# Differential attention in an fp32 diffusion backbone: the output product spread in groups between the pieces of the projections, with weight tiles of its own, and key copies issued by ScalarE

## Chip, cores, metric

One core of a Trainium2 chip. The metric is the device time of one execution in microseconds (us), lower is better.

## What is computed

The reference runs four layers over 512 latent tokens and 256 context tokens of width 1024: a Fourier mixer, differential attention, latent attention, a Fourier mixer again, each followed by an MLP. Everything is fp32. The change lies in layer 1, differential attention with 8 heads of 2 x 64 query and key channels and 128 value channels:

```python
def diff_attend(q1, q2, k1, k2, v, lam):
    scale = DIFF_HEAD_DIM ** -0.5
    s1 = jnp.einsum("bqhd,bkhd->bhqk", q1, k1).astype(jnp.float32) * scale
    s2 = jnp.einsum("bqhd,bkhd->bhqk", q2, k2).astype(jnp.float32) * scale
    p = jax.nn.softmax(s1, axis=-1) - lam * jax.nn.softmax(s2, axis=-1)
    return jnp.einsum("bhqk,bkhe->bqhe", p.astype(v.dtype), v)
...
    def finish(o):
        b, s = o.shape[:2]
        return (rms_norm(o, subln_g) * (1 - lam_init)).reshape(b, s, D_MODEL) @ w_o
```

Latent queries see all 768 keys, context queries the 256 context keys. `finish` normalises each head's output and multiplies by the output matrix `w_o`; the product, gated, is added to the stream x.

## The kernel before

Activations are kept transposed (channels on partitions, tokens on the free axis), 8 tiles of 128 channels. An fp32 product is made of three fp32r products: each operand is split into a high part (a cast on ScalarE, line 96) and a low part (a subtraction on VectorE, line 97), and hi x hi, hi x lo and lo x hi are summed in PSUM (lines 147 to 154). A weight tile therefore costs a load issued by SyncE (`wload`, line 99), a cast and a subtraction before TensorE can use it. In this stage there are two raw buffers of 512 columns for all loads, and a pool `dw` of eight weight tiles (four weights, high and low).

`diff` walks over the heads. Per head (work on TensorE in the order of the code):

- `S`: scores of one block of 128 queries against all keys, 8 products (12 with a context block), followed by the softmax on VectorE and ScalarE: maximum, exponential with its sum, reciprocals, and the difference of the two maps.
- `Tr`, `T2`: transposes of that difference (six blocks of 128), each split in high and low (`pth`, `ptl`).
- `PVa`: 18 products with the values of 256 queries; `PVb`: a product with ones for the sum of squares, then a chain over ScalarE and VectorE (`nt`, `nr`, `nu`) that ends in the normalised head output, `oh` (high, ScalarE) and `ol` (low, VectorE).

`last(hd - 1, ...)` finishes the second 256 queries of the former head after the first scores of the next one.

Between these stands filling work, which hides the softmax: the projections of values (`v`, for a pair of heads), queries (`q`) and keys (`k`) of later heads, and the output product of a finished pair (`wo`). It waits in a queue, `Fill`. `F(ns)` emits products from its front until that many nominal ns are filled; `need(name)` emits until all pieces of that name are out. Query and key projections come in two pieces (512 latent, 256 context columns, 24 products each); the values of a pair are one generator of 144 products; an output product of a pair is one generator of 96 products: for each of four weights two latent groups of 6 products (512 columns) and one context group of 12 (256 columns). In the queue it comes after the pair's values and the queries and keys of the next head. Each group ends in `accum` (line 368), a VectorE operation that adds it to x. All of this filling work goes through the PSUM tag `w` (`pw` in the profile) with two banks.

A latent key piece goes through the rotary embedding and then `put_k`: casts to `kh` on ScalarE (line 890), a copy of each half to the other 64 partitions by a DMA that GpSimd issues (line 891), and `kl` on VectorE (line 892).

TensorE's order is that of the code; the other engines' orders are made by a scheduler from the same program. TensorE, ScalarE, VectorE and the DMA queues each work in order.

In the rows, `pw<-hhi,g` is a query, `pw<-hhi,whi` a key, `pw<-whi,hhi` a value and `pw<-oh,whi` an output product; `ps` scores, `pu` transposes, value and ones products. Heads are counted from 0, pairs from 1 (heads 0 and 1) to 4.

Of the kernel before, what the change touches and what calls it, by code (L numbers as in the profile page):

```python
# [11 lines left out]
F32 = mybir.dt.float32  # L12
F32R = mybir.dt.float32r
# [31 lines left out]
def body(ctx: ExitStack, tc, a, out):  # L45
# [5 lines left out]
    def pool(es, name, bufs=1, **kw):  # L51
        return es.enter_context(tc.tile_pool(name=name, bufs=bufs, reuse_waits="tile", **kw))
# [39 lines left out]
    def rd(t):  # L92
        return t.bitcast(F32)

    def split(hi, lo, src):
        nc.scalar.copy(hi, src)  # L96
        nc.vector.tensor_sub(lo, src, rd(hi))  # L97
# [65 lines left out]
    class Fill:  # L163

        def __init__(self):
            self.q = []
            self.debt = 0.0
            self.open = False  # L170
            self.held = None

        def add(self, name, gens):
            self.q.extend([name, g, False] for g in gens)
# [14 lines left out]
        def step(self):  # L189
            if not self.open:  # L190
                self.prime(0)
                self.prime(1)
                self.open = True
            c = next(self.q[0][1], None)
            if c is None:
                self.q.pop(0)
                self.open = False
                return 0.0
            return c

        def run(self, ns):
            self.debt += ns
            while self.debt > 0 and self.q and self.q[0][0] != self.held:
                self.debt -= self.step()
            self.debt = min(self.debt, 0.0)

        def need(self, name):
# [3 lines left out]
        def drain(self):  # L211
            while self.q:
                self.step()

    def kview(w, k):
# [587 lines left out]
    def diff(l, h, nm):  # L803
        T = TT
        with ExitStack() as es:
            phase(es, "d", 2, {"s": (1024, 2), "u": (512, 2), "w": (512, 2)}, {"v": 1, "t": 1, "r": 1, "u": 1}, rw=512)
            cp = pool(es, "dc")
            wp = pool(es, "dw", 8)
            sp = pool(es, "ds")
            state["big"] = lambda: sp.tile([128, T], F32, name="big", tag="e0", bufs=2)  # L810
            cos = cp.tile([128, 512], F32, name="dcos")
# [26 lines left out]
                for m, (_, o) in enumerate(halves):  # L838
                    nc.gpsimd.tensor_copy(klz[i][m][o], zt[o])

            def gen_v(pr):
                wv = [wload(wp, a["dwv"][pr, i]) for i in range(4)]
                yield 0.0
                V[pr] = vh, vl = [sp.tile([128, 6, 256], F32R, name=n, tag="v", bufs=2) for n in ("vh", "vl")]
                for t0 in (0, 2, 4):
                    p = pt_("w")
                    for t in range(2):
                        i = 0
                        for k in range(KT):
                            hh, hl = tview(h[k], t0 + t)  # L850
                            wh, wl = tview(wv[k // 2], k % 2, 256)
# [31 lines left out]
            def put_k(hd):  # L883
                kh[hd] = [sp.tile([128, T], F32R, name=f"kh{m}", tag="kh", bufs=4) for m in range(2)]
                kl[hd] = klz[hd % 2]

                def put(t, c0, w_):
                    for m, (r, o) in enumerate(halves):
                        q = kh[hd][m][:, c0:c0 + w_]
                        nc.scalar.copy(q[r], t[r])  # L890
                        nc.gpsimd.dma_start(q[o], q[r])
                        nc.vector.tensor_sub(kl[hd][m][r, c0:c0 + w_], t[r], rd(q[r]))
                return put

# [16 lines left out]
            def gen_wo(pr, norm=None):  # L911
                ws = [wload(wp, a["dwo"][pr, b]) for b in range(2)]
                yield 0.0
                for b in range(4):
# [8 lines left out]
                    for j in range(2):  # L923
                        yield from mm3g(p[:, j * 256:], 2, lambda k: kview(w, k * 2 + j), lambda k: O[2 * pr + k], [(512, 256)], off=512)
                        accum(2 * b + j, 512, 256, p[:, j * 256:(j + 1) * 256], l, G_A)
                        if norm:
                            norm.feed(2 * b + j)

            def S(hd, c0, qi, cqi=None):

                s = [pt_("s"), pt_("s")]
                rows = [(c0 + qi * 128, [(0, 512, 0), (512, 256, 512)], 0, T,
                         [sp.tile([128, T], F32, name=f"e{m}", tag=f"e{m}", bufs=2 - m) for m in range(2)])]
                if cqi is not None:
                    rows.append((SL + cqi * 128, [(SL, SC, 768)], T, SC, [nacc[:, 0:256], nacc[:, 256:512]]))
                for q0, bl, _, _, _ in rows:
                    for m in range(2):
                        for k0, kw, o0 in bl:
                            o = s[m][:, o0:o0 + kw]
                            mm(o, qs[hd][m][:, q0:q0 + 128], kh[hd][m][:, k0:k0 + kw], True, False)  # L940
                            mm(o, qs[hd][m][:, q0:q0 + 128], kl[hd][m][:, k0:k0 + kw], False, True)
                for _, _, o0, w_, e in rows:
                    ri = []
                    for m in range(2):
                        mx = sp.tile([128, 1], F32, name="mx", tag="mx", bufs=4)
                        li = sp.tile([128, 1], F32, name="li", tag="li", bufs=4)
                        sv = s[m][:, o0:o0 + w_]
                        nc.vector.reduce_max(mx, sv, axis=AX.X, negate=True)  # L948
                        nc.scalar.activation(e[m], sv, AF.Exp, bias=mx, accum_out=li)
                        nc.vector.reciprocal(li, li)  # L950
                        ri.append(li)
                    nc.vector.tensor_mul(ri[1], ri[1], lam)
                    nc.scalar.activation(e[1], e[1], AF.Copy, scale=ri[1])
                    nc.vector.scalar_tensor_tensor(e[0], e[0], ri[0], e[1], op0=ALU.mult, op1=ALU.subtract)
                return s, [r[4][0] for r in rows]

            def Tr(e, c0, qi, b):
# [64 lines left out]
                F(1800)  # L1022
                PVb(hd, 256, st)

            fill.add("v0", [gen_v(0)])
            fill.add("q1", gens(1, 1))
            _, (e0, ec) = S(0, 0, 0, 0)
            for hd in range(8):
                p = hd // 2
                w = (5900, 3900, 7000, 7000, 7000, 7000, 7000, 5000)[hd]  # L1030
                F(500)
                if hd:
                    last(hd - 1, e3)
                    if hd % 2 == 0:
                        fill.front(f"v{p}", [gen_v(p)])
                        fill.add(f"wo{p - 1}", [gen_wo(p - 1)])
                F(w - 3500)
                _, (e1,) = S(hd, 0, 1)
                F(0.4 * w)
# [436 lines left out]
```

## Time and profile before

| | us |
|---|---|
| median of 3 runs | 2903.64 (2901.41 to 2911.14) |
| profiled execution | 2903.82 |
| its span, first to last instruction | 2902.0 |
| differential attention's heads, first scores to the last pair's output product | 757 to 1174 |
| TensorE busy in 720 to 1200 (480.0) | 418.38 |
| VectorE busy in the same | 378.94 |
| ScalarE busy in the same | 287.69 |

A window's row gives the busy time and the number of instructions of each engine in a stretch, then the clock granted to TensorE (1.00 is full). A timeline row gives start, duration, engine, line, operation, tiles and, in brackets, how long the engine had been idle and what ended that. A matmul's printed duration overlaps with the next one's; their spacing is the difference of their starts.

### The profile page before, as it was taken

The page shows a single profiled execution, that of the slowest core. Times are in us where ns is not written, and L with a number is a line of the kernel's source. Part 1 is how long each engine was busy: PE and PEld are TensorE (multiplying, and loading weights), DVE is VectorE, ACT ScalarE, POOL GpSimd, SP SyncE. Part 2 cuts the span into 40 slices and gives each one's busy share as a digit, 9 for nine tenths or more (in the row PEclk, how much of TensorE's full clock was granted, in tenths as well). Part 3 has the DMA queues.
Part 4 walks back from the last instruction along what each step waited for, and adds up shares of the span by engine and source line. Part 5 has one row for each costly group of instructions (what it writes and reads, how often), then busy time and mean ns, then how long its engine had stood idle before and what let it go on. Part 6 is the DMA issues. An engine that isn't in the chain of part 4 may idle for free.

```text
span 2902.0 us, 39734 instructions
## 1 busy us (share of the span) xinstructions
PE 2756.0 (95%) x15579; PEld 2377.6 (82%) x15579; DVE 1930.2 (67%) x3390; ACT 1290.8 (44%) x2325; POOL 159.9 (6%) x172
## 2 busy tenths in 40 slices
PE   8999999999799989799999998899899999999998
PEld 5788888888788878688888896788788888788887
DVE  7986666558697788875555448888785555664344
ACT  4542222234475656432332236777553334553342
POOL 0110000002110010100000011000100001100001
PEclk9999999999899999999999998999999999999999
DMA  9454333332111111253333210001265551232231
GB/s 319 148 181 131 110 116 104 107 95 82 48 48 45 40 47 39 96 161 114 120 113 116 88 37 32 22 23 37 71 224 175 163 173 55 81 116 95 80 110 51
DMA packets 93531, 291.12 MB, mean 100 GB/s; under 512 B 10624, under 2 KB 14880, under 8 KB 92832
## 3 DMA queue, kind: packets, MB, share of 16 engines
q1 hardware_dynamic: 90784, 285.44, 30.6%
q0 software_dynamic: 2560, 3.15, 0.5%
q8 instruction: 122, 2.00, 0.3%
q14 instruction: 65, 0.53, 0.1%
HBM read 283.29 MB, written 2.11 MB: 98 GB/s over the span
## 4 chain that ended last, share of the span: by engine, by line
PE 79%; DVE 13%; ACT 4%; issue 1%; DMA 1%; POOL 0%; POOLq 0%; SPq 0%; ACTq 0%; DVEq 0%
PE pw L140 70%; PE pu L140 5%; PE ps L140 3%; DVE x L371 2%; PE pu L797 1%; DVE ptl L97 1%; DVE mx L948 1%; DVE wlo L97 1%; DVE hlo L330 1%; DVE nu L328 1%; DVE mx L1280 1%; ACT e L1283 1%; DVE hlo L348 0%; PE pn L140 0%; ACT pth L96 0%
## 5 line engine op out<-in xcount | busy, mean ns | idle before, releaser
L96 ACT CAST whi<-raw 128x1024 fp32r<-128x1024 f32 (+1 forms) x322 | 308.2, 984 | 1064.7 <-PE pw L140 1012.0
L140 PE MATMUL pw<-hhi,wlo 128*128 128x512 f32 (+2 forms) x1680 | 588.0, 350 | 13.0 <-DVE wlo L97 13.0
L140 PE MATMUL pw<-hhi,whi 128*128 128x512 f32 (+2 forms) x1680 | 591.2, 352 | 3.2 <-ACT whi L96 1.5
L140 PE MATMUL pw<-hlo,whi 128*128 128x512 f32 (+2 forms) x1680 | 589.8, 351 | 0.0
L140 PE MATMUL pw<-ahi,whi 128*128 128x512 f32 (+1 forms) x1664 | 569.1, 342 | 0.0
L140 PE MATMUL pw<-alo,whi 128*128 128x512 f32 (+1 forms) x1664 | 567.6, 341 | 0.5 <-DVE alo L97 0.5
L140 PE MATMUL pw<-ahi,wlo 128*128 128x512 f32 (+1 forms) x1664 | 566.6, 340 | 0.0
L371 DVE SCALAR_TENSOR_TENSOR x<-pw,mod,x 128x512 f32<-128x512 f32 (+1 forms) x504 | 302.1, 623 | 283.0 <-PE pw L140 281.8
L97 DVE TENSOR_TENSOR wlo<-raw,whi 128x1024 fp32r<-128x1024 f32 (+1 forms) x322 | 362.2, 1140 | 164.1 <-ACT whi L96 163.5
L140 PEld LDWEIGHTS pw<-hhi,wlo 128*128 128x128 f32 x1680 | 319.4, 190 | 56.7 <-DVE wlo L97 13.6
L140 PEld LDWEIGHTS pw<-hhi,whi 128*128 128x128 f32 x1680 | 318.8, 190 | 47.7 <-ACT whi L96 1.9
L140 PEld LDWEIGHTS pw<-hlo,whi 128*128 128x128 f32 x1680 | 318.7, 190 | 42.4
L140 PEld LDWEIGHTS pw<-ahi,whi 128*128 128x128 f32 x1664 | 315.5, 190 | 37.0 <-issue 0.2
L140 PEld LDWEIGHTS pw<-alo,whi 128*128 128x128 f32 x1664 | 315.5, 190 | 36.2 <-DVE alo L97 0.7
L140 PEld LDWEIGHTS pw<-ahi,wlo 128*128 128x128 f32 x1664 | 315.1, 189 | 36.1
L264 DVE SCALAR_TENSOR_TENSOR raw<-raw,cb 128x1024 f32<-128x1024 f32 x176 | 216.0, 1228 | 117.2 <-DMA raw<-in_modw 115.5
L264 DVE SCALAR_TENSOR_TENSOR junk<-raw,cb 128x1024 bf16<-128x1024 f32 x96 | 117.2, 1220 | 70.6 <-DMA raw<-in_modw 68.4
L97 DVE TENSOR_TENSOR alo<-r,ahi 128x768 fp32r<-128x768 f32 (+2 forms) x134 | 105.8, 792 | 75.1 <-ACT ahi L96 74.8
L307 POOL TENSOR_TENSOR nacc<-nacc,nsq 128x256 f32<-128x256 f32 x70 | 52.9, 755 | 1751.5 <-ACT nsq L306 1751.2
L97 DVE TENSOR_TENSOR ptl<-pu,pth 128x384 fp32r<-128x384 f32 (+1 forms) x208 | 106.2, 539 | 37.5 <-ACT pth L96 36.0
L797 PE MATMUL pu<-ident,e 128*128 128x128 f32 x576 | 89.1, 280 | 21.1 <-ACT e L1283 11.8
L140 PE MATMUL pw<-hhi,g 128*128 128x512 f32 (+2 forms) x384 | 97.8, 337 | 3.9 <-DVE x L371 2.9
(327 smaller groups left out, 4259.4 us busy)
## 6 DMA issues: line engine op xcount, KB each, us to landing
raw<-in_w SPq DMA_DIRECT2D x252, 512.0 KB, 4.1
raw<-in_modw SPq DMA_DIRECT2D x176, 512.0 KB, 3.7
wm<-in_msh SPq DMA_DIRECT2D x32, 256.0 KB, 6.0
raw<-in_fw SPq DMA_DIRECT2D x10, 512.0 KB, 4.3
cb<-scr SPq DMA_DIRECT2D x4, 1024.0 KB, 5.3
raw<-in_dwk SPq DMA_DIRECT2D x16, 256.0 KB, 2.6
raw<-in_dwq SPq DMA_DIRECT2D x16, 256.0 KB, 2.7
raw<-in_dwv SPq DMA_DIRECT2D x16, 256.0 KB, 2.8
```

Of the source, the lines that this page charges most:

```text
L96: nc.scalar.copy(hi, src)
L97: nc.vector.tensor_sub(lo, src, rd(hi))
L140: r = nc.tensor.matmul(o, lhsT, rhs, start=start, stop=stop)
L264: nc.vector.scalar_tensor_tensor(o, m, 1.0, cb[:, v * 1024:(v + 1) * 1024], op0=ALU.mult, op1=ALU.mult, accum_out=mcol(mod[l, ch], v, k))
L307: nc.gpsimd.tensor_tensor(nacc[:, c0:c0 + w], nacc[:, c0:c0 + w], s, op=ALU.add)
L328: nc.vector.scalar_tensor_tensor(u, xs, am, r, op0=ALU.mult, op1=ALU.mult)
L330: nc.vector.scalar_tensor_tensor(lo, u, sh, rd(hi), op0=ALU.add, op1=ALU.subtract)
L371: nc.vector.scalar_tensor_tensor(xs, src, mcol(mod[l, ch], 0 if c0 < SL else 1, n), xs, op0=ALU.mult, op1=ALU.add)
L797: nc.tensor.transpose(t[:, i * 128:(i + 1) * 128], p[:, (k0 + i) * 128:(k0 + i + 1) * 128], ident)
L948: nc.vector.reduce_max(mx, sv, axis=AX.X, negate=True)
L1280: nc.vector.reduce_max(mx, s[:, :T], axis=AX.X)
L1283: nc.scalar.activation(et, s[:, :T], AF.Exp, bias=mx, scale=MLA_SCALE)
```

## The change

Five edits, all in layer 1:

1. The output product of pairs 1 to 3 leaves the queue and becomes a side generator (`side_wo`) of 12 groups. Whenever a piece of the queue has ended, two whole groups (for the third pair one) are emitted; if the queue is held or empty, `F` emits groups too; before head 3's and head 5's values product, and at the end, what is left is emitted at once (`end_side`). It starts right after `last` of the odd head. The fourth pair's product, after the last head, is as before.
2. The values of a pair become three pieces of 48 products, so that there are more ends of pieces.
3. The side's weights have a pool of their own, `dx`, of two tiles (one weight, high and low), loaded when the first group of the weight is emitted.
4. The key copies are issued by ScalarE instead of GpSimd; the DMA scratch of GpSimd is halved.
5. The two row sums of a softmax share a tile, with one reciprocal for both.

The numbers `w` that `F` is given are changed for head 7 (5000 to 3000).

```diff
@@ class Fill
+            self.side = iter(())
+            self.rate = 2
...
             if c is None:
                 self.q.pop(0)
                 self.open = False
-                return 0.0
+                return sum(next(self.side, 0.0) for _ in range(self.rate))
             return c

         def run(self, ns):
             self.debt += ns
-            while self.debt > 0 and self.q and self.q[0][0] != self.held:
-                self.debt -= self.step()
+            while self.debt > 0:
+                if self.q and self.q[0][0] != self.held:
+                    self.debt -= self.step()
+                else:
+                    c = next(self.side, None)
+                    if c is None:
+                        break
+                    self.debt -= c
             self.debt = min(self.debt, 0.0)
...
+        def end_side(self):
+            for _ in self.side:
+                pass
@@ diff
+            wx = pool(es, "dx", 2)
...
-            def gen_v(pr):
-                wv = [wload(wp, a["dwv"][pr, i]) for i in range(4)]
-                yield 0.0
...
+            def gens_v(pr):
...
+                return [piece(t0) for t0 in (0, 2, 4)]
...
-                        nc.gpsimd.dma_start(q[o], q[r])
+                        nc.scalar.dma_start(rd(q)[o], rd(q)[r])
...
+            def side_wo(pr):
+                for b in range(4):
+                    w = wload(wx, a["dwo"][pr, b])
+                    for j in range(2):
+                        yield wo_lat(pr, w, b, j)
+                    yield wo_cx(pr, w, b)
+
+            def wo_lat(pr, w, b, j):
+                p = pt_("w")
+                mm3(p, 2, lambda k: kview(w, k * 2 + j), lambda k: O[2 * pr + k], [(0, 512)])
+                accum(2 * b + j, 0, 512, p, l, G_A)
+                return 1360.0
+
+            def wo_cx(pr, w, b):
+                p = pt_("w")
+                for j in range(2):
+                    mm3(p[:, j * 256:], 2, lambda k: kview(w, k * 2 + j), lambda k: O[2 * pr + k], [(512, 256)], off=512)
+                    accum(2 * b + j, 512, 256, p[:, j * 256:(j + 1) * 256], l, G_A)
+                return 1440.0
...
-                    ri = []
+                    li = sp.tile([128, 2], F32, name="li", tag="li", bufs=4)
...
-                        nc.vector.reciprocal(li, li)
-                        ri.append(li)
-                    nc.vector.tensor_mul(ri[1], ri[1], lam)
...
+                    nc.vector.reciprocal(li, li)
+                    nc.vector.tensor_mul(li[:, 1:2], li[:, 1:2], lam)
...
-                w = (5900, 3900, 7000, 7000, 7000, 7000, 7000, 5000)[hd]
+                w = (5900, 3900, 7000, 7000, 7000, 7000, 7000, 3000)[hd]
...
-                        fill.front(f"v{p}", [gen_v(p)])
-                        fill.add(f"wo{p - 1}", [gen_wo(p - 1)])
+                        fill.front(f"v{p}", gens_v(p))
+                        fill.side = side_wo(p - 1)
+                        fill.rate = 2 if p < 3 else 1
...
                 if hd in (3, 5):
-                    fill.need(f"wo{p - 1}")
+                    fill.end_side()
```

How this stands on the engines, at three places. First TensorE in head 2, where the latent key piece (`pw` from `hlo`, `hhi`) ends behind the ones product of head 1's second half. Before:

```order
L140 MATMUL pw_7692<-hhi_1751,whi_7652 128x512
L140 MATMUL pu_7798<-nt_7817,ones_79 128x256 [waits Activation_49]
L140 MATMUL pw_7692<-hlo_1752,whi_7652 128x512
L140 MATMUL pw_7692<-hhi_1751,wlo_7653 128x512
L140 MATMUL pw_7881<-hhi_1737,whi_7646 128x256
L140 MATMUL pw_7881<-hlo_1738,whi_7646 128x256
```

After (`oh_7083` is head 0's output, `oh_7538` and `ol_7539` are head 1's):

```order
L140 MATMUL pw_7671<-hhi_1751,whi_7631 128x512
L140 MATMUL pu_7773<-nt_7792,ones_79 128x256 [waits Activation_49]
L140 MATMUL pw_7671<-hlo_1752,whi_7631 128x512
L140 MATMUL pw_7671<-hhi_1751,wlo_7632 128x512
L140 MATMUL pw_7838<-oh_7083,whi_7834 128x512
L140 MATMUL pw_7838<-ol_7084,whi_7834 128x512
L140 MATMUL pw_7838<-oh_7083,wlo_7835 128x512
L140 MATMUL pw_7838<-oh_7538,whi_7834 128x512 [waits Activation_49]
L140 MATMUL pw_7838<-ol_7539,whi_7834 128x512 [waits DVE_49]
L140 MATMUL pw_7838<-oh_7538,wlo_7835 128x512
```

Where the context key piece followed, the first two output groups now stand in between (12 products), and their fourth and fifth products wait for head 1's output.

Second ScalarE in head 4, from the end of the same chain for head 3 (`oh_8722`, `oh_8806`: its output). Before:

```order
L890 CAST kh0_8895<-pw_9083 64x256 [waits DMASW6_49,DMASW4_49,PE_49]
L890 CAST kh0_8895<-qt_9071 64x512 [waits DVE_49]
L890 CAST kh1_8896<-qt_9071 64x512 [waits DMASW7_49,DMASW5_49]
L96 CAST whi_9130<-raw_9128 128x512 [waits DMAHW7_49]
L96 CAST oh_8722<-nu_9068 128x256 [waits DVE_49]
L96 CAST g_9153<-raw_9151 128x512 [waits DMAHW0_49]
L890 CAST kh1_8896<-pw_9083 64x256 [waits DVE_49]
```

After (`whi_9081` is a value weight, `whi_9106` the first output weight of the pair):

```order
L911 CAST kh0_8879<-pw_9034 64x256 [waits PE_49]
L912 DMA kh0_8879<-kh0_8879 64x256 [waits Activation_49]
L911 CAST kh0_8879<-qt_9022 64x512 [waits DVE_49]
L911 CAST kh1_8880<-qt_9022 64x512
L912 DMA kh0_8879<-kh0_8879 64x512 [waits DMAHW6_49,Activation_49]
L912 DMA kh1_8880<-kh1_8880 64x512 [waits DMAHW7_49,Activation_49]
L96 CAST oh_8806<-nu_9019 128x256 [waits DVE_49]
L96 CAST whi_9081<-raw_9079 128x512 [waits DMAHW3_49]
L911 CAST kh1_8880<-pw_9034 64x256 [waits DVE_49]
L96 CAST whi_9106<-raw_9104 128x512 [waits DMAHW5_49]
```

The key copies have entered the row, the value weight's cast has moved behind the head's output, and the output weight's cast is the last of all.

Third TensorE where a context group ends and the next weight's first group follows. Before (second weight of a pair, in head 3):

```order
L140 MATMUL pw_8447<-oh_7557,whi_8286 128x256
L140 MATMUL pw_8447<-ol_7558,whi_8286 128x256
L140 MATMUL pw_8447<-oh_7557,wlo_8287 128x256
L140 MATMUL pw_8497<-oh_7090,whi_8292 128x512
L140 MATMUL pw_8497<-ol_7091,whi_8292 128x512
```

After (the same weight, now in head 2):

```order
L140 MATMUL pw_7934<-ol_7539,whi_7834 128x256
L140 MATMUL pw_7934<-oh_7538,wlo_7835 128x256
L140 MATMUL pw_7955<-oh_7083,whi_7951 128x512 [waits DVE_49,Activation_49]
L140 MATMUL pw_7955<-ol_7084,whi_7951 128x512
L140 MATMUL pw_7955<-oh_7083,wlo_7952 128x512 [waits DVE_49]
```

The next weight's first product waits for its cast and its bank, the third for its subtraction; before, neither waits.

More of the change, by code (lines that the diff above doesn't have):

```diff
@@ L213, in drain @@
                 self.step()
+            self.end_side()
+        def end_side(self):
+            for _ in self.side:
+                pass
     def kview(w, k):
@@ L839, in diff, with piece @@
                     nc.gpsimd.tensor_copy(klz[i][m][o], zt[o])
-            def gen_v(pr):
-                wv = [wload(wp, a["dwv"][pr, i]) for i in range(4)]
-                yield 0.0
-                V[pr] = vh, vl = [sp.tile([128, 6, 256], F32R, name=n, tag="v", bufs=2) for n in ("vh", "vl")]
-                for t0 in (0, 2, 4):
+            def gens_v(pr):
+                st = []
+                def piece(t0):
+                    if not st:
+                        st.extend(wload(wp, a["dwv"][pr, i]) for i in range(4))
+                        V[pr] = [sp.tile([128, 6, 256], F32R, name=n, tag="v", bufs=2) for n in ("vh", "vl")]
+                    yield 0.0
+                    vh, vl = V[pr]
                     p = pt_("w")
@@ L850, in gen_v @@
                             hh, hl = tview(h[k], t0 + t)
-                            wh, wl = tview(wv[k // 2], k % 2, 256)
+                            wh, wl = tview(st[k // 2], k % 2, 256)
                             for u_, v_ in ((hh, wh), (hh, wl), (hl, wh)):
@@ L942, in S @@
                 for _, _, o0, w_, e in rows:
-                    ri = []
+                    li = sp.tile([128, 2], F32, name="li", tag="li", bufs=4)
                     for m in range(2):
                         mx = sp.tile([128, 1], F32, name="mx", tag="mx", bufs=4)
-                        li = sp.tile([128, 1], F32, name="li", tag="li", bufs=4)
                         sv = s[m][:, o0:o0 + w_]
                         nc.vector.reduce_max(mx, sv, axis=AX.X, negate=True)
-                        nc.scalar.activation(e[m], sv, AF.Exp, bias=mx, accum_out=li)
-                        nc.vector.reciprocal(li, li)
-                        ri.append(li)
-                    nc.vector.tensor_mul(ri[1], ri[1], lam)
-                    nc.scalar.activation(e[1], e[1], AF.Copy, scale=ri[1])
-                    nc.vector.scalar_tensor_tensor(e[0], e[0], ri[0], e[1], op0=ALU.mult, op1=ALU.subtract)
+                        nc.scalar.activation(e[m], sv, AF.Exp, bias=mx, accum_out=li[:, m:m + 1])
+                    nc.vector.reciprocal(li, li)
+                    nc.vector.tensor_mul(li[:, 1:2], li[:, 1:2], lam)
+                    nc.scalar.activation(e[1], e[1], AF.Copy, scale=li[:, 1:2])
+                    nc.vector.scalar_tensor_tensor(e[0], e[0], li[:, 0:1], e[1], op0=ALU.mult, op1=ALU.subtract)
                 return s, [r[4][0] for r in rows]
@@ L1023, in last @@
                 PVb(hd, 256, st)
-            fill.add("v0", [gen_v(0)])
+            fill.add("v0", gens_v(0))
             fill.add("q1", gens(1, 1))
@@ L1464 @@
     arrays = _layout({k: np.asarray(v) for k, v in inputs.items()})
-    nc = bacc.Bacc("TRN2", target_bir_lowering=False, num_devices=1, dynamic_dma_scratch_size=8192)
+    nc = bacc.Bacc("TRN2", target_bir_lowering=False, num_devices=1, dynamic_dma_scratch_size=4096)
     feed, aps = {}, {}
```

## The prediction

> **What bounds the kernel now.** I read the page's busy shares and chain first, then the differential-attention stage by head (windows cut at the first score product of each head), then TensorE's waits there, and last the timelines at the places that the change moves.
>
> ```profile
> PE 2756.0 (95%) x15579; PEld 2377.6 (82%) x15579; DVE 1930.2 (67%) x3390; ACT 1290.8 (44%) x2325; POOL 159.9 (6%) x172
> PE 79%; DVE 13%; ACT 4%; issue 1%; DMA 1%; POOL 0%; POOLq 0%; SPq 0%; ACTq 0%; DVEq 0%
> ```
>
> TensorE carries the chain, so the change can only act through TensorE's idle time in this one stage. Columns below: stretch, its length, busy time of PE, PEld, DVE, ACT, POOL, granted clock, DMA. The rows are heads 1 to 6, then head 7 up to its last scores.
>
> ```profile
> 804.20:843.05 38.85, 36.53 (x216) 31.00 (x216) 36.28 (x81) 29.32 (x68) 4.74 (x6) 0.96 0.18 45
> 843.05:897.39 54.34, 51.66 (x360) 47.29 (x360) 43.27 (x92) 35.99 (x81) 4.69 (x6) 1.00 0.18 47
> 897.39:956.91 59.52, 53.02 (x316) 45.59 (x315) 47.13 (x100) 32.59 (x72) 4.67 (x6) 1.00 0.15 42
> 956.91:1010.87 53.96, 49.97 (x350) 45.43 (x349) 43.10 (x90) 35.18 (x80) 5.29 (x6) 1.00 0.17 48
> 1010.87:1069.92 59.05, 52.97 (x316) 45.53 (x315) 46.63 (x100) 32.58 (x72) 4.66 (x6) 1.00 0.15 43
> 1069.92:1124.18 54.26, 50.05 (x351) 45.58 (x350) 43.82 (x92) 36.51 (x83) 5.29 (x6) 1.00 0.19 52
> 1124.18:1158.46 34.28, 29.65 (x179) 26.00 (x178) 28.47 (x65) 19.34 (x45) 0.00 (x0) 0.95 0.08 24
> ```
>
> In heads 2 to 6 TensorE is the fullest engine. In head 1, which has the least product work, VectorE is as full (36.28 of 38.85, 93%). Where TensorE waits:
>
> ```profile
> PE pw L140 <- DVE x L371: 16.7, 16, 2.2
> ```
>
> From 880 to 1160 us the output products wait 16.7 us in 16 waits (1.04 each) for the accumulation into x that frees their bank.
>
> **The parts that take time away.** Three pairs' output products (96 per pair) are respread; pair 3, after the last head, is left alone. Prices:
>
> ```profile
> 940.25:948.82 8.57, 8.57 (x50) 1.00 0.42 107
> L371 DVE SCALAR_TENSOR_TENSOR x<-pw,mod,x 128x512 f32<-128x512 f32 (+1 forms) x60 | 36.3, 612 | 9.7 <-PE pw L140 9.1
> ```
>
> The first is a whole query projection, 24 products of 512 columns and 24 of 256, with two cut ones at its edges: 8.4 us for 48, that is 0.233 and 0.117 each. A pair's output is twice that, 16.8 us.
>
> Heads 3 and 5: by the order, 9 products of 512 columns of a pair (2.1 us) stand in the even head now and the other 14.7 us in the odd one; the changed order has none in heads 3 and 5. So 59.52 falls to 44.8 by the work alone. Head 1 tells what a head without output takes: 38.85, with 12 key products of 512 columns fewer (2.8 us more in heads 3 and 5), and with 3.3 us at half clock (rows below) that cost 1.5. That gives 40.2. VectorE agrees: 47.13 less some 14 accumulations of 0.612 and two weight subtractions is about 37, at head 1's 93% 39.8. Gain beyond the work: 44.8 - 40.2 = 4.6, and 59.05 - 14.7 - 40.2 = 4.2. Sum -8.8 (bounds 0, if 44.8 stays, and -12).
>
> Head 7: it keeps 48 output products (8.4 us) of the 14.5 it has. VectorE loses about 7 accumulations of 0.612, 4.2 of its 28.47; at the present 83% the 34.28 become 29.3, at head 1's 93% 26.1. I take the nearer row, its own: -5.0 (bounds 0 and -8.2). The tail behind it stays, since nothing is left to fill it in either order.
>
> Even heads: three of the 16 waits lie at their ends, 3 x 1.04 = 3.1. And the value pieces of heads 4 and 6 now start before their weights are split (rows of pair 2, below): from the last key product at 967.63 to the scores at 973.00 there are 5.25 us for 21 value products (2.5), 2.8 lost in each. In the new order those weights are ready before the piece starts. Sum -8.7.
>
> Together -22.5.
>
> **The parts that add time.** The first output group of a pair now follows the key piece at once, right behind the ones product of the odd head's second half. In pair 1 it has only the head's normalised output to wait for (4th product on):
>
> ```profile
> 852.52 0.59 PE L140 MATMUL pu<-nt,ones 128*128 128x256 f32 x2
> ...
> 856.72 1.26 ACT L890 CAST kh<-qt 64x512 fp32r<-64x512 f32 x2 [1.18 <-DVE qt L870]
> 858.53 0.40 ACT L96 CAST oh<-nu 128x256 fp32r<-128x256 f32 x1
> ...
> 857.55 0.47 DVE L993 SCALAR_TENSOR_TENSOR nu<-nu,gs,nr 128x256 f32<-128x256 f32 x1
> 859.37 0.42 DVE L97 TENSOR_TENSOR ol<-nu,oh 128x256 fp32r<-128x256 f32 x1
> ```
>
> Two key products of 0.233 and the ones product's own place follow; the group would start at 853.4 and reach its fourth product at 854.1. The cast of the output (oh) ends at 858.93 now, behind one weight cast that the new order has later; without that, and with nu 0.6 earlier, it ends at about 858.4. Wait 4.3, and 0.5 more for ol: 4.8.
>
> In pairs 2 and 3 the group's weight cast stands behind oh, a value-weight cast and a key cast on ScalarE (the order shows it), so the first product already waits:
>
> ```profile
> 966.01 0.59 PE L140 MATMUL pu<-nt,ones 128*128 128x256 f32 x2
> 967.63 0.28 PE L140 MATMUL pw<-hhi,wlo 128*128 128x256 f32 x1
> 973.00 0.39 PE L140 MATMUL ps<-kh,qs 128*128 128x512 f32 x1
> ...
> 971.92 0.68 DVE L97 TENSOR_TENSOR wlo<-raw,whi 128x512 fp32r<-128x512 f32 x1
> 972.52 0.48 DVE L993 SCALAR_TENSOR_TENSOR nu<-nu,gs,nr 128x256 f32<-128x256 f32 x1
> ...
> 973.04 0.41 ACT L96 CAST oh<-nu 128x256 fp32r<-128x256 f32 x1 [1.80 <-DVE nu L993]
> 973.99 0.37 ACT L890 CAST kh<-pw 64x256 fp32r<-64x256 f32 x1
> ```
>
> ```profile
> L96 ACT CAST whi<-raw 128x512 fp32r<-128x512 f32 x47 | 29.0, 623 | 19.6 <-PE pw L140 12.3 <-DMA raw<-in_dwk 3.8 <-DMA raw<-in_dwo 2.1
> L97 DVE TENSOR_TENSOR wlo<-raw,whi 128x512 fp32r<-128x512 f32 x48 | 32.6, 685 | 8.7 <-ACT whi L96 8.3
> ```
>
> The wlo at 971.92 moves behind oh, so nu ends at 972.4 and oh at 972.9; then 0.62, 0.37 and 0.62 on ScalarE: the first product starts at about 974.5 where TensorE was free at 967.75. The low half follows at about 975.4, 0.4 more. 7.1 in each of two pairs, with 4.8: +19.0. The key copies' issues stand ahead of oh on ScalarE too; the 1.80 of idle time there covers two or three of them. Both bounds: with idle queues the same chain is
>
> ```profile
> 1173.74 0.70 PE L140 MATMUL pu<-nt,ones 128*128 128x256 f32 x2 [0.74 <-ACT nu L985]
> ...
> 1177.78 0.50 PE L140 MATMUL pw<-oh,whi 128*128 128x512 f32 x1 [2.65 <-ACT oh L96]
> ```
>
> 4.04 from ones to product: 2.5 in pair 1 and, with 1.61 of casts, 3.9 in the others, 10.3 in all. With today's times unshifted: 21.9. I keep 19.0, since the queues there are today's.
>
> Half clock behind waits (the last column but two is the clock; the first row is from the stage's start, the second from head 1):
>
> ```profile
> 739.89:745.70 5.81, 5.81 (x14) 4.55 (x15) 0.55 (x1) 0.00 (x0) 0.00 (x0) 0.50 0.27 90
> 803.80:807.10 3.30, 2.90 (x9) 2.52 (x10) 3.17 (x7) 1.65 (x4) 0.00 (x0) 0.50 0.01 4
> 1131.50:1134.80 3.30, 3.30 (x17) 3.30 (x16) 1.12 (x3) 1.64 (x6) 0.00 (x0) 0.50 0.00 0
> ...
> 1130.19 0.39 PE L140 MATMUL pw<-oh,whi 128*128 128x256 f32 x1 [2.15 <-DVE x L371]
> ```
>
> A wait of 2.15 us was followed by 3.3 us at half clock (1.7 lost); the longest stretch, with TensorE busy in all of it, was 5.81 (2.9 lost). All three first groups wait longer than 2.15: 1.7 + 2.3 + 2.3, the two long ones between the rows: +6.3 (bounds 5.1 and, with a fourth, 11.6). [...]
>
> Weight tiles of their own: one weight in flight (two tiles). Where a context group ends and the next weight's group follows at once, the cast waits for the former: 0.62 + 0.69 + about 0.2 of hand-over, less two products of 0.233, 1.05 each. That is so three times (heads 2, 4, 4), a half time in head 7 (0.4), and 2.5 at the first in head 2, where the load itself waits until the value weights ahead have left the two raw buffers: +6.0 (bounds 4.2 and 11).
>
> A second group behind a piece needs the bank the piece has just filled: a cast and a subtraction, about 1.5, against 1.4 of the first group, 0.1 to 0.9 in six places; and the group's lump uses up the fill, so that eight transposes in head 2 and a few ones products stand without cover, under 1 each: +4.0 (bounds 0 and 7).
>
> Softmax and key copies:
>
> ```profile
> L950 DVE RECIPROCAL li<-li 128x1 f32<-128x1 f32 x96 | 14.6, 156 | 8.0 <-ACT e L949 5.8 <-ACT nacc L949 1.7
> L891 POOL DMA_DIRECT2D kh<-kh x32 | 16.9, 530 | 39.7 <-ACT kh L890 37.2 <-PE ps L140 1.8
> ```
>
> 48 reciprocals fewer are 7.5 us of VectorE, under 1 a head, and the last one stays in its chain: 0. The copies put 32 x at most 0.53 = 17 us on ScalarE, 2.1 a head, where even head 1 leaves 9.5 idle; heads use their keys a head later, so landing is covered: 0 (bounds -2 and +4; without that idle time the exponentials would be late). Behind a waiting issue stand casts of oh, hence the term above.
>
> **Sum.** -22.5 + 19.0 + 6.3 + 6.0 + 4.0 = +12.8. The profiled execution took 2903.8 (span 2902.0, 1.8 around it), 0.2 above the median of the runs: 2916.6, given as 2916.
>
> **Rivals.**
> A, faster: ScalarE and VectorE empty their queues while TensorE stands, as head 1's 93% suggests they can. Then the first groups cost 10.3, the clock 3.4 (two waits), the tiles 4.2, nothing else, and head 7 gives 8.2 (3.2 more): 2903.8 - 25.7 + 17.9 = 2896. It is under the old time as soon as the new waits stay under 25.7. For it: the waits on x are VectorE's lateness, not TensorE's. Against: in-order queues with the weight cast behind the head's chain. 0.17.
> B, no change: VectorE is drained only at the first groups (10.3 + 5.1), the tiles cost 6.0 and the rest 2: 23.4 against 22.5, 2905. 0.18.
> C, dearer: odd heads and head 7 do not shrink beyond their work, because VectorE or the chain from scores to transposes sets them and ScalarE now has the copies too: 2916.6 + 13.8 = 2930. For it: head 7's tail, slow without fill. 0.15.
> That the groups would not move at all is excluded by the order.
>
> **Numbers.** The forecast keeps 0.50, with 2907 to 2924 as its own range. 0.3% (8.7 us) is about what a measurement of this kernel can tell from no change. Faster than 2895: somewhat less than half of A and tails, 0.11. Within: the rest of A, all of B mostly, and the quarter of the forecast below 2912: 0.34. Slower: 0.55. The range reaches to A and C: 2896 to 2932.
>
> **What would show it.** Right: in the profile after, waits of output products on x shrink from 16.7 to some 4 between the same heads; waits of pw on ACT oh or whi of about 5, 7 and 7 us appear with granted clock 0.5 behind them; heads 3 and 5 take 39 to 41 us, the even ones 70 to 78. Wrong: first-group waits of 3 to 4 us, heads 3 and 5 at 45 or at 36, or ScalarE's issue of a copy far over 0.5 us, which would put exponentials late and TensorE's transposes with them.

## Result and profile after

The changed kernel takes 2940.36 us (median of 4 runs, 2938.98 to 2942.91), the kernel before 2904.82 in the same session (4 runs, 2901.41 to 2911.14). The ratio is 1.0121, 95% interval 1.0105 to 1.0136: slower, as forecast (2916), but by nearly three times as much and above the range (2932). The profiled execution took 2942.9, its span 2940.7, which is 38.7 more than before.

The page's busy shares and the start of its chain, after:

```profile
PE 2773.1 (94%) x15579; PEld 2384.4 (81%) x15579; DVE 1927.5 (66%) x3342; ACT 1289.7 (44%) x2325; POOL 142.5 (5%) x140
PE 78%; DVE 13%; ACT 5%; issue 2%; DMA 2%; POOL 0%; ACTq 0%; POOLq 0%; SPq 0%; DVEq 0%
```

TensorE executes as many products as before (15579). Its busy time is 17 us more, much of it products at half clock (below), which count as longer (with 512 columns their starts lie 0.43 us apart at 853.9 to 855.6, against 0.23 at 847.4 to 847.8); the other 22 us are idle.

The same windows by head, after (columns as in the prediction: length, PE, PEld, DVE, ACT, POOL, clock, DMA). The rows are heads 1 to 6, then head 7 up to its last scores:

```profile
797.87:836.92 39.05, 36.83 (x216) 31.30 (x216) 35.49 (x75) 29.70 (x69) 2.66 (x2) 0.96 0.16 45
836.92:922.18 85.26, 71.16 (x446) 61.09 (x447) 53.64 (x104) 36.70 (x81) 2.56 (x2) 0.98 0.13 36
922.18:964.95 42.77, 38.18 (x231) 32.50 (x230) 35.96 (x76) 30.94 (x71) 2.60 (x2) 1.00 0.16 46
964.95:1054.04 89.09, 72.10 (x437) 62.88 (x436) 58.33 (x109) 39.74 (x87) 3.18 (x2) 0.90 0.14 41
1054.04:1096.55 42.51, 38.06 (x231) 32.14 (x230) 34.50 (x70) 27.39 (x65) 2.67 (x2) 1.00 0.13 34
1096.55:1164.75 68.20, 58.27 (x390) 52.93 (x388) 45.46 (x90) 34.56 (x79) 3.19 (x2) 0.95 0.11 30
1164.75:1192.82 28.07, 23.52 (x143) 20.40 (x141) 25.29 (x54) 20.73 (x48) 0.00 (x0) 0.94 0.18 57
```

Against before, heads 2 to 7 change by +30.9, -16.8, +35.1, -16.5, +13.9 and -6.2. All that stands before head 2 gains 6.1 and what follows the last scores loses 4.3. The products only change heads: priced at 0.233 and 0.117 each, a pair moves 14.7 us from its odd to its even head, and the third pair 6.1 from head 7 to head 6. Length less products (transposes are priced at 0.117 too, which drops out of the differences), the time lost in each head, is then:

| head | lost before | lost after | difference |
|---|---|---|---|
| 2, 4, 6 | 4.4, 6.3, 6.4 | 20.6, 26.8, 14.3 | +44.6 |
| 3, 5 | 8.7, 8.2 | 6.6, 6.3 | -4.0 |
| 7 | 7.5 | 7.4 | -0.1 |

So the loss lies in the even heads, which have the groups, and the odd heads give little back. What TensorE waits for from head 2 to the last scores (us in total, times, longest):

```profile
PE pw L140 <- ACT whi L96: 16.9, 6, 6.9
PE pw L140 <- DVE x L385: 11.5, 13, 1.1
...
PE pw L140 <- DVE wlo L97: 4.8, 3, 2.6
PE pw L140 <- ACT oh L96: 4.2, 1, 4.2
```

(L385 is the accumulation, L371 before.) The waits on x fall from 16.7 only to 11.5, and the waits on casts of weights and output are new. The first groups of the three pairs, from TensorE's timeline:

```profile
852.39 0.50 PE L140 MATMUL pw<-oh,whi 128*128 128x512 f32 x1 [4.16 <-ACT oh L96]
853.30 0.79 PE L140 MATMUL pw<-ol,whi 128*128 128x512 f32 x1 [0.41 <-DVE ol L97]
...
982.61 0.79 PE L140 MATMUL pw<-oh,whi 128*128 128x512 f32 x1 [6.85 <-ACT whi L96]
...
1114.01 0.80 PE L140 MATMUL pw<-oh,whi 128*128 128x512 f32 x1 [6.54 <-ACT whi L96]
```

That is 18.0 us of waits. Why the second takes 6.85 is seen on ScalarE and VectorE (rows of both; TensorE was free at 975.8):

```profile
978.34 1.40 DVE L913 TENSOR_TENSOR kl<-qt,kh 64x512 fp32r<-64x512 f32 x2
979.77 0.48 DVE L1032 SCALAR_TENSOR_TENSOR nu<-nu,gs,nr 128x256 f32<-128x256 f32 x1
...
980.29 0.41 ACT L96 CAST oh<-nu 128x256 fp32r<-128x256 f32 x1 [1.85 <-DVE nu L1032]
980.60 0.61 ACT L96 CAST whi<-raw 128x512 fp32r<-128x512 f32 x1
981.24 0.37 ACT L911 CAST kh<-pw 64x256 fp32r<-64x256 f32 x1
981.94 0.62 ACT L96 CAST whi<-raw 128x512 fp32r<-128x512 f32 x1 [0.33 <-DMA raw<-in_dwo]
```

Two key subtractions hold the head's last normalisation (nu) back, ScalarE's cast of the output stands waiting for nu, and the group's own weight cast is three places behind that cast. This is the queue that the prediction described.

Half clock (the last column but two) goes with each long wait, and with one turn of the weight tiles (the hand-over of the tiles from one weight to the next) in head 4 and one in head 7:

```profile
853.16:856.57 3.41, 3.27 (x8) 2.59 (x9) 0.84 (x2) 0.00 (x0) 0.00 (x0) 0.50 0.21 46
979.45:986.28 6.83, 3.67 (x9) 2.86 (x10) 4.04 (x8) 1.91 (x4) 0.00 (x0) 0.50 0.53 151
1037.48:1047.72 10.24, 8.86 (x33) 7.79 (x34) 3.06 (x6) 3.07 (x8) 0.00 (x0) 0.50 0.08 27
1112.57:1119.40 6.83, 5.39 (x17) 4.53 (x18) 4.24 (x7) 2.58 (x5) 0.00 (x0) 0.50 0.44 119
1180.84:1184.25 3.41, 3.41 (x13) 2.93 (x12) 2.43 (x5) 1.64 (x3) 0.00 (x0) 0.50 0.50 154
```

In the first four stretches TensorE is busy for 21.2 us, half of which, an estimated 10.6, is lost. The fifth, in head 7, costs the 1.7 that head 7 lost to one such stretch before (1131.50 in the prediction's rows), so it adds nothing. The longest follows this turn in head 4, the last weight of the pair (rows of TensorE, ScalarE and VectorE):

```profile
1035.00 0.50 PE L140 MATMUL pw<-oh,whi 128*128 128x512 f32 x1 [1.58 <-ACT whi L96]
...
1038.34 0.79 PE L140 MATMUL pw<-oh,wlo 128*128 128x512 f32 x1 [2.61 <-DVE wlo L97]
...
1033.51 0.94 ACT L992 ACTIVATE e<-e,li 128x768 f32<-128x768 f32 x1 [1.78 <-DVE li L991]
1034.35 0.60 ACT L96 CAST whi<-raw 128x512 fp32r<-128x512 f32 x1
...
1035.12 1.01 DVE L993 SCALAR_TENSOR_TENSOR e<-e,li,e 128x768 f32<-128x768 f32 x1
1036.16 1.41 DVE L901 SCALAR_TENSOR_TENSOR qs<-qt,qs 64x512 fp32r<-64x512 f32 x2
1037.60 0.69 DVE L97 TENSOR_TENSOR wlo<-raw,whi 128x512 fp32r<-128x512 f32 x1
```

The two tiles hold one weight, high and low, so the next weight's cast comes only after the last products of the former; here it stands behind a softmax on ScalarE, and the low half behind that softmax and a query on VectorE.

### The profile page after: what moved, and what is told of

It reads as the page before. It is cut to its first block, busy times and chain, and to the rows that moved or that the text cites. A ratio compares the mean times of both kernels' runs of the same rounds, so it can differ in the third digit from the quotient of the medians.

```text
span 2940.7 us, 39635 instructions
## 1 busy us (share of the span) xinstructions
PE 2773.1 (94%) x15579; PEld 2384.4 (81%) x15579; DVE 1927.5 (66%) x3342; ACT 1289.7 (44%) x2325; POOL 142.5 (5%) x140
## 4 chain that ended last, share of the span: by engine, by line
PE 78%; DVE 13%; ACT 5%; issue 2%; DMA 2%; POOL 0%; ACTq 0%; POOLq 0%; SPq 0%; DVEq 0%
PE pw L140 69%; PE pu L140 5%; PE ps L140 3%; DVE ptl L97 1%; DVE x L385 1%; PE pu L811 1%; DVE mx L988 1%; DVE wlo L97 1%; DVE mx L1320 1%; ACT e L1323 1%; DVE hlo L344 1%; DVE nu L342 1%; ACT whi L96 1%; ACT pth L96 1%; ACT e L989 0%
## 5 line engine op out<-in xcount | busy, mean ns | idle before, releaser
L385 DVE SCALAR_TENSOR_TENSOR x<-pw,mod,x 128x512 f32<-128x512 f32 (+1 forms) x504 | 302.4, 622 | 292.7 <-PE pw L140 290.0
L140 PE MATMUL pw<-hhi,g 128*128 128x512 f32 (+2 forms) x384 | 104.0, 353 | 5.0 <-DVE x L385 2.8
```

Source lines behind the costliest of these rows:

```text
L140: r = nc.tensor.matmul(o, lhsT, rhs, start=start, stop=stop)
L385: nc.vector.scalar_tensor_tensor(xs, src, mcol(mod[l, ch], 0 if c0 < SL else 1, n), xs, op0=ALU.mult, op1=ALU.add)
```

## Experiments

Medians are compared through their ratio to runs of the kernel before on the same chip in the same session (its medians there 2905.9, 2906.9 and 2907.5). The changed kernel is 1.0121.

| kernel | median us | ratio | 95% interval |
|---|---|---|---|
| b45 | 2901.96 | 0.9983 | 0.9974 to 0.9993 |
| unspread | 2899.76 | 0.9975 | 0.9965 to 0.9986 |
| late | 2919.83 | 1.0046 | 1.0031 to 1.0061 |
| cx | 2937.14 | 1.0107 | 1.0090 to 1.0124 |
| pre4 | 2934.75 | 1.0103 | 1.0088 to 1.0118 |
| late_cx | 2910.98 | 1.0015 | 1.0006 to 1.0025 |
| late_pre | 2900.78 | 0.9973 | 0.9962 to 0.9984 |
| all3 | 2893.06 | 0.9956 | 0.9941 to 0.9971 |
| all4 | 2892.30 | 0.9944 | 0.9929 to 0.9958 |
| h7 | 2936.86 | 1.0104 | 1.0090 to 1.0117 |
| bcx | 2892.90 | 0.9949 | 0.9936 to 0.9963 |
| uncx | 2887.69 | 0.9921 | 0.9904 to 0.9939 |

**b45: the two small edits alone, in the kernel before** (key copies and softmax).

```
-                        nc.gpsimd.dma_start(q[o], q[r])
+                        nc.scalar.dma_start(rd(q)[o], rd(q)[r])
...
+                    nc.vector.reciprocal(li, li)
```

> The kernel before with only two of the edits: key copies issued by ScalarE, and one reciprocal for both maps. Theory 1 (these cost nothing): 2902 to 2906. Rival (ScalarE's issues make exponentials and the casts of the output late, in every head): 8 heads x 1 to 2 us, 2912 to 2920.

0.9983: a little under the old time, so the loss is not in these edits. The first head shows where they help; its windows, before and in b45:

```profile
757.50:804.20 46.70, 41.27 (x287) 37.91 (x285) 32.98 (x70) 28.71 (x66) 2.31 (x3) 0.96 0.16 44
```

```profile
754.76:797.77 43.01, 39.77 (x286) 36.51 (x284) 32.17 (x64) 28.74 (x65) 1.29 (x1) 1.00 0.16 48
```

3.7 us go there, and the changed kernel has the same 43.0. An estimated 1.7 of it is a stretch at half clock (766.18 to 769.59, TensorE busy for 3.34 us) that b45 does not have, hence 0.96 against 1.00. Which of the two edits does it was not separated.

**unspread: the change with the spreading alone taken back**, with four weight tiles of its own (all kernels with four such tiles halve the DMA scratch of GpSimd once more).

```
-                        fill.side = side_wo(p - 1)
-                        fill.rate = 2 if p < 3 else 1
+                        fill.add(f"wo{p - 1}", [gen_wo(p - 1, wt=wx)])
...
-                    fill.end_side()
+                    fill.need(f"wo{p - 1}")
```

> The changed kernel with the spreading alone taken back: the output products of a pair stand in the queue of fill again, behind the even head's projection pieces and issued product by product, with weight tiles of their own (four); the split value pieces, the key copies on ScalarE, the single reciprocal and the smaller fill of head 7 stay. Theory 1 (the loss is the spreading): 2902 to 2908. Rival (the split value pieces, the smaller fill of head 7 or tiles of their own carry a part of the 35 us): 2912 to 2925.

0.9975, below the expected 2902. So the spreading, with the two tiles it came with, carries all of the loss: 1.0121 - 0.9975 = 1.5% (42 us) hangs on it. The split value pieces, the copies, the softmax and the smaller fill of head 7 together do no harm.

**late: the groups handed over later in the even head**, after its third scores.

```
-                        fill.side = side_wo(p - 1)
-                        fill.rate = 2 if p < 3 else 1
+                        nxt = side_wo(p - 1)
...
                 _, (e2, ec) = S(hd, 256, 0, 1)
+                if hd and hd % 2 == 0:
+                    fill.side = nxt
+                    fill.rate = 2 if p < 3 else 1
```

> The changed kernel, but a pair's groups are handed over after the first value piece's scores of the even head instead of at its start, so that other products stand where the first group waited for the head's output and the weight cast. Theory 1 (the loss is made of the waits of the first groups): the three waits of 4.2 + 0.4, 6.9 and 6.5 us go, 18 in all, with some 8 us of half clock behind them; 4 to 8 us come back because the groups now stand closer together: 2941 - 18 to 22 = 2919 to 2923. Rival (the waits are only moved, because ScalarE and VectorE are behind in the even heads anyway): the same time is lost at the next group, 2935 to 2941.

1.0046, 20.5 us less: theory 1 holds, and its rival, that the waits only move, falls. The three waits of the first groups, 18.0, are gone; waits on weight casts remain, 4.5 us of them before value products (2.27 in each of heads 4 and 6) and three of 0.59 before output products (TensorE's waits, head 2 to the last scores):

```profile
PE pw L140 <- ACT whi L96: 6.3, 5, 2.3
```

**cx: both halves of a context group first, then both accumulations.**

```
                 for j in range(2):
                     mm3(p[:, j * 256:], 2, ..., [(512, 256)], off=512)
+                for j in range(2):
                     accum(2 * b + j, 512, 256, p[:, j * 256:(j + 1) * 256], l, G_A)
```

> The changed kernel, but a context group issues the products of both its halves and only then the two accumulations, so that the second half's products no longer stand behind the first half's accumulation. Theory 1 (the waits of output products on x that were left, 13.5 us in heads 2 to 7, come from the two halves sharing one tile): 11 groups x 0.6 to 1.1 us = 7 to 12 us go, of which the later reader of the bank takes back a part: 2931 to 2936. Rival (VectorE is late, and the next group waits for it instead): 2939 to 2943.

1.0107: its interval overlaps that of the change, so its 3 us are within what can be told. Both expectations miss. The waits on x do go, but about half of that time comes back at the tiles (TensorE's waits, head 2 to the last scores):

```profile
PE pw L140 <- ACT whi L96: 17.1, 6, 6.7
PE pw L140 <- DVE wlo L97: 9.4, 5, 4.1
...
PE pw L140 <- DVE x L385: 1.0, 1, 1.0
```

x goes from 11.5 (not the 13.5 of the expectation) to 1.0 and wlo from 4.8 to 9.4, with one turn of 4.1. Groups that finish sooner reach a next weight that is not ready.

**pre4: four tiles, weights loaded two ahead.**

```
-            wx = pool(es, "dx", 2)
+            wx = pool(es, "dx", 4)
...
+                ws = [wload(wx, a["dwo"][pr, b]) for b in range(2)]
+                yield 0.0
```

> The changed kernel with four weight tiles instead of two and the weights loaded two ahead. Theory 1 (the turns of the two tiles cost what the trace shows: 0.7 + 0.1 + 0.7 + 0.5 + 0.6 + 1.6 + 2.6 + 1.7 us, and part of the 10 us at half clock in head 4): 8 to 12 us go, 2929 to 2933. Rival (two casts ahead of the head's chain on ScalarE and VectorE make the first groups later by 1 to 2 us each, and fill the raw buffers of the value weights): 2938 to 2946.

1.0103, 5.6 us less in the medians, with intervals that overlap: smaller than theory 1 said. The turns go, but the first groups of pairs 1 and 2 still wait as long (4.2 on oh, 6.5 on whi), and the waits on x grow from 11.5 to 17.1:

```profile
PE pw L140 <- DVE x L385: 17.1, 18, 2.4
PE pw L140 <- ACT whi L96: 8.8, 2, 6.5
```

The edit does a second thing. The added `yield 0.0` uses up one emission of the generator: at the first end of a piece pairs 1 and 2 emit one group instead of two, and pair 3, which emits one at a time, none, so its first group stands behind a whole value piece. Its wait of 6.54 is gone, and a value product of head 6 waits 2.27 on its weight instead. So pre4, and each kernel below with four tiles and spread groups, measures the tiles and this small delay together.

**Two and three cures together.** Kernels late_cx, late_pre and all3 combine the edits above.

> The changed kernel with the three cures together: groups handed over after the first value piece's scores, four weight tiles loaded two ahead, both accumulations of a context group behind its products. One by one they took 20.5, 5.6 and 3.2 us off. If they are separate places: 2940.4 - 29 = 2911. If the late start already took the turns of the tiles with it (theory of one cause, the groups' lateness): 2917 to 2920. If they help each other by leaving VectorE room: below 2906.

> The changed kernel with the late start and the two accumulations behind both halves, the two weight tiles kept. The three cures together took 47.3 us where one by one they took 20.5 + 3.2 + 5.6 = 29.3; 18 are shared. Alone, these two would sum to 2916.7. Theory 1 (VectorE is full in the even heads and each cure lets it catch up, so any two help each other): 2903 to 2911. Theory 2 (the late start brings the tiles' turns close together, and the extra lies between the late start and the tiles): 2915 to 2918.

> The changed kernel with the late start and four weight tiles loaded two ahead, the accumulations as they were. The sum of the single gains is 2914.3. Theory 1 (every pair of cures helps): 2903 to 2910. Theory 2 (late start and tiles belong together): 2896 to 2901, and the accumulations' order then gives its 3 to 6 us on top. If all the extra lies with the accumulations: 2913 to 2916.

One by one late, cx and pre4 take 0.75, 0.14 and 0.18% off; all3 takes 1.65, not 1.07, and came below the 2906 of its third theory. late_pre takes 1.48, which is 0.55 more than its parts, in theory 2's range. late_cx takes 1.06, 0.17 more, which is no more than the intervals allow; its 2910.98 lies at the edge of theory 1's range and not in theory 2's. So most of what they share lies between the late start and the edit of pre4, as theory 2 said; whether a part lies with the accumulations stays open. The place is the even heads. Heads 4 and 6 in late:

```profile
956.47:1024.73 68.26, 60.35 (x401) 53.19 (x400) 50.05 (x98) 37.09 (x83) 3.20 (x2) 1.00 0.14 41
...
1077.05:1139.43 62.38, 55.42 (x373) 50.20 (x371) 45.01 (x87) 34.57 (x80) 3.18 (x2) 0.97 0.12 32
```

and in late_pre:

```profile
957.58:1020.37 62.79, 58.49 (x396) 52.18 (x394) 50.48 (x101) 38.07 (x86) 3.19 (x2) 1.00 0.18 49
1070.42:1124.49 54.07, 51.44 (x366) 47.36 (x365) 43.03 (x88) 34.48 (x80) 3.19 (x2) 1.00 0.15 37
```

5.5 and 8.3 us less. (Head 6 in late_pre holds a little less product work, 49.7 against 51.3.) In late the value products of head 4 wait for their second weight; TensorE, and ScalarE ahead of it:

```profile
972.90 0.39 PE L140 MATMUL pw<-whi,hhi 128*128 128x256 f32 x1 [2.27 <-ACT whi L96]
...
971.92 0.40 ACT L96 CAST oh<-nu 128x256 fp32r<-128x256 f32 x1 [1.85 <-DVE nu L1032]
972.23 0.61 ACT L96 CAST whi<-raw 128x512 fp32r<-128x512 f32 x1
```

In late_pre that cast stands ahead of the key casts and of the cast of the output, and the value products do not wait:

```profile
968.96 0.60 ACT L96 CAST whi<-raw 128x512 fp32r<-128x512 f32 x1
969.47 1.26 ACT L911 CAST kh<-qt 64x512 fp32r<-64x512 f32 x2
...
974.47 0.41 ACT L96 CAST oh<-nu 128x256 fp32r<-128x256 f32 x1
```

So in late_pre the casts of the value weights have also moved in the queue. Why the order comes out so, and how much of the shared 0.55% is this, how much the turns and how much the later groups of pre4's edit, the runs do not tell apart.

**h7: the third pair's groups all in head 7**, whose fill is as large as before.

```
-                        fill.side = side_wo(p - 1)
-                        fill.rate = 2 if p < 3 else 1
+                        if p < 3:
+                            fill.side = side_wo(p - 1)
...
+                if hd == 7:
+                    fill.side = side_wo(2)
```

> The changed kernel, but the third pair's twelve groups all stand in head 7, with the fill of that head as it was before. Theory 1 (the loss of heads 6 and 7, 8.3 us against before, is the first group's wait of 6.5 us and the half clock behind it): 2930 to 2934. Rival (head 7's VectorE becomes the bound with all 24 accumulations): 2938 to 2945, head 7 longer than 44.2 by more than the 8.4 us of products that it gains.

1.0104: between the two expectations, and its interval overlaps that of the change, so it settles little. The trace has heads 6 and 7 up to the last scores at

```profile
1098.11:1152.05 53.94, 49.20 (x342) 44.80 (x340) 38.40 (x77) 31.68 (x74) 3.19 (x2) 0.97 0.12 32
1152.05:1187.30 35.25, 27.89 (x165) 23.20 (x165) 29.30 (x62) 22.61 (x53) 0.00 (x0) 1.00 0.07 23
```

Head 6 is back at its old length (54.3), without the 6.54 us wait, while head 7 goes up by 7.2, with a wait on wlo of 1.76 among others: 7.1 less for both, in one execution.

**bcx: the kernel before with only the order of the accumulations changed**, in all four pairs.

```
                     for j in range(2):
                         yield from mm3g(p[:, j * 256:], 2, ..., [(512, 256)], off=512)
+                    for j in range(2):
                         accum(2 * b + j, 512, 256, p[:, j * 256:(j + 1) * 256], l, G_A)
```

> The kernel before with one edit that is in no version so far: a context group issues both halves' products and only then both accumulations (all four pairs, the last one too). Theory 1 (the waits on x come from the two halves sharing a tile): about 11 of 24 us of waits on x go, of which VectorE's lateness takes back half: 2897 to 2901. Rival (nothing is gained, the next group waits instead): 2903 to 2908.

0.9949, 14 us off, more than expected. The wait (head 2 to the last scores, 16.7 before) and heads 3 and 5 (59.52 and 59.05 before):

```profile
PE pw L140 <- DVE x L371: 4.0, 4, 1.4
```

```profile
898.71:953.97 55.26, 52.33 (x317) 45.45 (x315) 46.54 (x100) 32.55 (x72) 4.67 (x6) 1.00 0.16 46
...
1007.92:1062.90 54.98, 52.14 (x317) 45.34 (x316) 46.45 (x100) 32.60 (x72) 4.67 (x6) 1.00 0.16 46
```

4.3 and 4.1 us, and the last pair's product, alone at the end, falls from 30.9 to 25.6 from its first product to its last. VectorE's work in heads 3 and 5 is nearly the same (46.5 us against 47.1 and 46.6), so it was the order that made TensorE wait, not the amount of VectorE's work. In the changed kernel the rows of one such pair of halves (TensorE, and the first half's accumulation) are

```profile
997.05 0.39 PE L140 MATMUL pw<-oh,whi 128*128 128x256 f32 x1 [1.08 <-DVE x L385]
...
996.52 0.47 DVE L385 SCALAR_TENSOR_TENSOR x<-pw,mod,x 128x256 f32<-128x256 f32 x1
```

The first half's last product starts at 995.69, the accumulation at 996.52, and the second half's products at its end. VectorE does have a share in the length of this wait: a value subtraction (995.91 to 996.60) stands ahead of the accumulation. The shortest waits of this kind take 0.58. The second half's products write other columns of the same tile and still wait, 1.08 us in these rows.

**all4 and uncx: the best of each kind.** all4 is all3 with the last pair's accumulations reordered too, uncx is unspread with the reorder of bcx.

> The kernel of three cures with the accumulations of the last pair (the one that is not spread) behind both halves too. In the kernel before that edit took 14 us in four pairs, so a quarter, 3.5, if it is worth the same in each pair: 2893.1 - 3.5 = 2889.6. The last pair stands alone with nothing beside it, so it may be worth more: down to 2885. If it changes nothing there: 2893.

> The changed kernel with the spreading taken back (as in the run of that name) and the accumulations behind both halves in all four pairs. If the gains add: 2899.8 - 14 = 2886. If the own weight tiles and the order of accumulations remove the same waits: 2892 to 2896. Compared with the three cures plus the last pair it says whether spreading, once cured, is worth anything.

all4: 0.9944 against 0.9956 for all3, intervals overlapping. uncx: 0.9921, 20 us under the kernel before and the fastest here; the gains of unspread (0.25%) and of bcx (0.51%) add. Spreading with every cure (all4) is not faster than no spreading (uncx): the intervals overlap, but all four runs of uncx (2882.3 to 2890.1) lie below all four of all4 (2891.1 to 2893.9). late_pre equals unspread (0.9973 and 0.9975). Cured, the spreading costs little or nothing, and nothing shows that it gains.

## Why the prediction was right in sign and wrong in size

The sign stood, and so did the mechanism behind it: new waits at the first groups take more than the odd heads give back. On the lost time of heads 2 to 7 the forecast was +12.8; it came out at +40.5. Of the stretches outside them, forecast at 0, the one before gained 6.1 and the one after lost 4.3. (The "pair 3" that the prediction leaves alone is the fourth pair.)

- **First groups: right.** Predicted 4.8 + 7.1 + 7.1 = 19.0; measured 4.16 + 0.41, 6.85 and 6.54, 18.0. late took them away and 20.5 us with them.
- **Half clock: too small.** Predicted 6.3 for three stretches; it came to an estimated 10.6 in four. The one more, with the turn of 2.61 us in head 4, is the longest; the working had named it as a bound (11.6) and not taken it.
- **Turns of the tiles: near in sum by luck, not in shape.** Predicted 6.0, in bounds of 4.2 to 11; the waits on whi and wlo beyond the first groups add up to 16.9 - 13.4 + 4.8 = 8.3 us, 6.6 of it in the even heads. The first turn of head 2 took 0.7, not 2.5, and the one of head 7 1.7, not 0.4. The price of a cast and a subtraction with idle queues (1.05) roughly holds for the second turn of head 2 (1.2) and one of head 4 (0.6), and fails where a softmax is ahead of the cast: 4.2 for one.
- **Waits on x: the step that failed.** The text read them as VectorE's lateness and let them fall from 16.7 to about 4, 3.1 of that in the even heads. They stayed at 11.5, and the even heads' share rose from 3.9 to 9.5: +5.6 in place of -3.1. The cause was in the code: the two halves of a context group write one tile, and the first is accumulated ahead of the second's products (bcx). Spreading carries that along with the group. Of the misses this is the largest in the account of waits, 8.7; it is not what the term is worth alone, since cx took these waits down to 1.0 and won at most a few us.
- **Head 7: an error of bookkeeping.** Its fall from 34.28 to 29.3 was entered as a gain of 5.0. It came out at 28.07, but 6.1 us of products had only gone to head 6, so the gain is 0.1. For heads 3 and 5 the moved work had been set apart, for head 7 not.
- **Odd heads: half.** 42.77 and 42.51 instead of 40.2: -4.0 instead of -8.8. The waits that remain there, 4.5 us in each of the two heads, are on ptl, nu, qs and kl: the chain of scores, transposes and casts that rival C had named. That it set the missing 4.8 was not tested.
- **Value weights in the even heads: right.** Of their 5.6 predicted, about 5.0 came: those waits (1.0 on wlo, 0.5 on qt, in each of heads 4 and 6, and the half-fed stretch behind them) are gone in the profile after; 3.0 of it were waits, and the rest is an estimate.
- **The rest without cover:** 4.0 predicted; 44.6 - 18.0 - 10.6 - 6.6 (turns in the even heads) - 5.6 (x) + 5.0 leaves 8.8. Waits of PV products and transposes on ptl in the even heads rise by 3.1 (2.3 to 5.4); the others are too short to be told apart, so the larger part of this term stays open.
- **Softmax and copies: better than predicted.** Predicted 0, at best -2; measured 0.17% faster (b45), 4.9 us, most of it in head 0.

Against the forecast: even heads 18.0 too low, head 7 and the odd heads 4.9 and 4.8 too low, which is the difference of 27.7. Under "what would show it", the first-group waits came; the odd heads (42.8 and 42.5) just missed 39 to 41, x at 4 did not come, and the even heads took 85, 89 and 68 us, not 70 to 78. The range was too narrow because its upper end was rival C alone, with every other term at its forecast. With all terms at their own upper bounds (no gain in the odd heads and head 7) and the even heads' gain at -8.7, the sum is -8.7 + 21.9 + 11.6 + 11 + 7 = +42.8, or 2946. The gain of the even heads, with x in it, had no bound at all.

## What to carry to other kernels

Before a wait is put down to a late engine, look whether the waiting group and the one that is drained share a tile: here moving one loop took 14 us, more than any respreading. Work that is moved to fill gaps brings its own chain (cast of the operand, weights, turn of tiles); place it where its inputs have long been ready, and give it enough tiles that no cast falls behind a softmax. When work moves between two stages, set it apart in both before calling a shorter stage a gain.

## What was not expected of the hardware

The five stretches at half clock lasted 3.41, 6.83, 10.24, 6.83 and 3.41 us, as the rows above show. The one that went with the wait of 2.61 us in head 4 cost an estimated 4.4 us more (half of 8.86 busy). It lasted 10.24 us with TensorE busy for 8.86 of them, the one in head 2 only 3.41 with TensorE busy for 3.27; what made the former so long the runs do not settle.

Nor do they tell how much of a wait brings half clock. In the 3.41 us ahead of each of the five stretches TensorE was busy for 0.50, 0.00, 0.73, 0.00 and 1.70 us. The last of these (1177.43 to 1180.84, ahead of head 7's stretch) held a single wait of 1.71 us. In the kernel before, a single wait of 1.71 us (up to 953.22, TensorE busy for 1.70 us from 950.50 to 953.91) was followed by full clock (1.00 from 953.91 to 957.32).
